# Block 2's gated delta rule: 32x32 triangular inverses by four doublings on TensorE instead of substitution in blocks of 16 on VectorE

## The chip, the cores and the metric

The kernel runs on one core of a Trainium2 chip. The metric is the device time of one execution in microseconds (us). Engines are named as in the profile: PE (TensorE, its weight loads apart as PEld), DVE (VectorE), ACT (ScalarE), POOL (GpSimd), SP (SyncE, which issues most DMAs). Each engine takes its instructions in the order of its own queue.

## The reference, cut to what matters

Two blocks follow each other. The change is in the first mixer of the second block, a chunked gated delta rule with 4 heads, 768 tokens and two directions:

```python
    a_mat = jnp.where(tri_strict, jnp.einsum('nbhid,nbhjd->nbhij', kb, kc) * decay, 0.0)
    eye = jnp.eye(cs, dtype=jnp.float32)
    t_mat = lax.linalg.triangular_solve(eye + a_mat, jnp.broadcast_to(eye, a_mat.shape),
                                        left_side=True, lower=True, unit_diagonal=True)
    u = jnp.einsum('nbhij,nbhjd->nbhid', t_mat, vb)
    w = jnp.einsum('nbhij,nbhjd->nbhid', t_mat, kb * jnp.exp(gcum)[..., None])
...
    def step(s, xs):
        u_i, w_i, qg_i, kd_i, at_i, ge_i = xs
        v_new = u_i - jnp.einsum('bhck,bhkv->bhcv', w_i, s)
        o_i = jnp.einsum('bhck,bhkv->bhcv', qg_i, s) + jnp.einsum('bhij,bhjv->bhiv', at_i, v_new)
        s = s * ge_i[..., None, None] + jnp.einsum('bhck,bhcv->bhkv', kd_i, v_new)
        return s, o_i
```

So each chunk needs the inverse of a unit triangular matrix. The kernel works in chunks of 128 tokens (6 of them), which gives 6 matrices of 128x128 for each head and direction. Beside the delta rule the same mixer has a gated MLP (`gmlp`) on the same input, and both results go through one output projection.

## The kernel before

`ab_mixer` holds the whole stage. Its big products are `dense` calls: three matmuls (`mm` or `mf` from `hh,whi`, `hl,whi` and `hh,wlo`, line L277) for each 128x128 piece of a weight, on 512 and 256 columns. The weight pieces come by DMA (`raw`) and are split by ACT (`whi`, L263) and DVE (`wlo`, L264).

The four heads run one after the other (`gdn_head`). A head first makes q, k and v by `dense`. Then `gdn_dir` runs twice, forward and backward. Each call of `gdn_dir` builds the decay-weighted matrices (L1507 on PE, L1508 and L1509 on DVE; the matrix to invert is `aT`, kept in the buffer `gkb`), calls `gdn_inv`, and then steps through 6 chunks (`gdn_chunk`: on PE L1595, L1598 and L1603, each of which waits for DVE or ACT on the step before). That makes 8 calls of `gdn_inv`.

`gdn_inv` takes the 32x32 diagonal blocks of all 6 matrices into one tile `c32` (4 blocks on the 128 partitions, 6 matrices on the free axis) and has `inv32` invert them; what follows (L1564 to L1586) joins them to 128x128 on PE. `inv32` masks the blocks to 16x16, and solves those by substitution: 15 rounds of three DVE instructions,

```python
            nc.vector.stream_shuffle(sh[:, :, W], x16[:, :, W], [j] * 16 + [16 + j] * 16)
            nc.vector.tensor_tensor(pr[:, :, W], sh[:, :, W], a[:, :, j:j + 1].broadcast_to([128, U, n]), op=ALU.mult)
            nc.vector.tensor_tensor(x16[:, :, W], x16[:, :, W], pr[:, :, W], op=ALU.subtract)
```

(L889, L890, L891). One doubling then joins two 16-blocks into a 32-block: a DVE transpose (L900), 24 small matmuls on PE (L907, `goff`), an ACT copy (L909), 24 more matmuls (L907, `gw`), a DVE subtraction (L910), and a last transpose (L911). In this text 24 such matmuls are called a piece; the trace shows each of them as two passes, so a piece is 48 rows of the trace.

`gmlp` depends on nothing of the delta rule. It is written after the heads, but a scheduler sets the order of each engine's instructions, and it puts the dense matmuls of `gmlp` (`mf`) and of the next head (`mm`) between the steps of the delta rule, and at the end those of the output projection. That order is fixed when the program is built.

After the heads, the tiles `ma` (the parts of the mixed result) come back by DMA, are multiplied by the gates (POOL, L1316), and are split into `hh` and `hl` (ACT L398, DVE L399) for the output projection.

Of the kernel before, what the change touches and what calls it, by code (L numbers as in the profile page):

```python
# [49 lines left out]
def _consts():  # L50
    p = np.arange(128)
    c = {}
# [1 line left out]
    c["bones"] = (p[:, None] // 64 == p[None, :] // 64) * 1.0  # L54
    c["ones"] = np.ones((128, 128))
    vals = [1e-5, 1e-6, 64e-5, 1e-12]
    c["m16"] = np.stack([p % 32 < 16, p % 32 >= 16], 1)
    c["i16"] = (p[:, None] % 16 == np.arange(16)[None]) * 1.0
    t32 = np.arange(32)
    for d in range(2):  # L60
        up = (p[:, None] % 32 < 16) & (t32[None] >= 16)
        c[f"off{d}"] = up if d == 0 else (p[:, None] % 32 >= 16) & (t32[None] < 16)
    c["cc"] = np.broadcast_to(np.array(vals), (128, len(vals)))
    s = p % 64
    t = np.arange(64)
    for d in range(2):
# [10 lines left out]
    s5, t5 = p[:, None] % 32, np.arange(32)[None]  # L77
# [4 lines left out]
    i = np.arange(64)  # L82
# [6 lines left out]
def _consts2():  # L89
    p = np.arange(128)  # L90
    c = {}
    t = np.arange(128)
    for d in range(2):
        le = (p[:, None] <= t[None]) if d == 0 else (p[:, None] >= t[None])
        c[f"mneg{d}"] = np.where(le, 0.0, -1e30)
        t32 = np.arange(32)
        c[f"gst{d}"] = ((p[:, None] % 32 < t32[None]) if d == 0 else (p[:, None] % 32 > t32[None])) * 1.0
    return _pack(c)


# [97 lines left out]
class B:  # L198
# [666 lines left out]
        nc.vector.transpose(flat(t), flat(x))  # L865
        return x, t

    def inv32(self, c32, U, dd, pool, pre, bank):


        nc = self.nc

        def bc(n, w):
            return self.C(n).rearrange("p (o t) -> p o t", o=1).broadcast_to([128, U, w])

        def tl(n, w, tag=None):
            return pool.tile([128, U, w], F32, tag=pre + (tag or n), name=pre + n)

        m0, m1 = self.C("m16", 0, 1), self.C("m16", 1, 2)
        off = tl("off", 32)  # L880
        nc.gpsimd.tensor_tensor(off, c32, bc(f"off{dd}", 32), op=ALU.mult)
        a, x16, sh, pr = tl("a16", 16), tl("x16", 16), tl("sh", 16), tl("pr", 16)
        nc.gpsimd.tensor_copy(x16, bc("i16", 16))
        nc.vector.tensor_scalar(a, c32[:, :, 0:16], m0, None, op0=ALU.mult)
        nc.vector.scalar_tensor_tensor(a, c32[:, :, 16:32], m1, a, op0=ALU.mult, op1=ALU.add)
        for j in (range(15, 0, -1) if dd == 0 else range(15)):
            W = slice(j, 16) if dd == 0 else slice(0, j + 1)
            n = W.stop - W.start
            nc.vector.stream_shuffle(sh[:, :, W], x16[:, :, W], [j] * 16 + [16 + j] * 16)  # L889
            nc.vector.tensor_tensor(pr[:, :, W], sh[:, :, W], a[:, :, j:j + 1].broadcast_to([128, U, n]), op=ALU.mult)  # L890
            nc.vector.tensor_tensor(x16[:, :, W], x16[:, :, W], pr[:, :, W], op=ALU.subtract)  # L891
        x = tl("x32", 32)
        nc.vector.tensor_scalar(x[:, :, 0:16], x16, m0, None, op0=ALU.mult)
        nc.vector.tensor_scalar(x[:, :, 16:32], x16, m1, None, op0=ALU.mult)
        t, w = tl("t32", 32), tl("w16", 32, "c32")
# [4 lines left out]
        nc.vector.transpose(flat(t), flat(x))  # L900
        ps = self.psum(bank, (128, 2, U, 32))
        for n in range(2):
            for u in range(U):
                for i in range(4):
                    R = slice(32 * i, 32 * i + 32)
                    l, r = (off, t) if n == 0 else (w, x)
                    nc.tensor.matmul(ps[R, n, u], l[R, u], r[R, u], start=True, stop=True, tile_position=(32 * i, 32 * i))  # L907
            if n == 0:
                nc.scalar.copy(w, ps[:, 0])  # L909
        nc.vector.tensor_tensor(x, x, ps[:, 1], op=ALU.subtract)  # L910
        nc.vector.transpose(flat(t), flat(x))  # L911
        return x, t

# [623 lines left out]
    def gdn_inv(self, aT, dd):  # L1537

        nc = self.nc
        f1 = self.f1  # L1540
        Q = [slice(32 * i, 32 * i + 32) for i in range(4)]
        c32 = f1.tile([128, 6, 32], F32, name="gc32")
        m = self.C2(f"gst{dd}").rearrange("p (o t) -> p o t", o=1).broadcast_to([128, 6, 32])
        for i in range(4):
            eng = nc.gpsimd if i % 2 else nc.vector
            eng.tensor_tensor(c32[Q[i]], aT[Q[i], :, Q[i]], m[Q[i]], op=ALU.mult)
        x, t = self.inv32(c32, 6, dd, f1, "g", "rsc")
        X = self.f2.tile([128, 6, 128], F32, name="gX")
        tn = f1.tile([128, 6, 64], F32, name="gtn")
        w = f1.tile([128, 6, 32], F32, tag="gc32", name="gw32")  # L1550
# [9 lines left out]
        ps = self.psum("rsc", (128, 2, 6, 32))  # L1560
        prs = [(2 * r + S, 2 * r + D_) for r in range(2)]
        for c in range(6):
            for s, e in prs:
                nc.tensor.matmul(ps[Q[e], 0, c], aT[Q[s], c, Q[e]], t[Q[s], c], start=True, stop=True,  # L1564
                                 tile_position=(32 * s, 32 * e))
# [215 lines left out]
```

## Time and profile before

| what | value |
|---|---|
| median of 3 runs | 2731.26 us (2726.3 to 2732.86) |
| profiled execution, its own time | 2736.78 us |
| its span, first to last instruction | 2735.0 us |
| mean granted TensorE clock | 0.947 of full |
| calls of `inv32` | 8, between 1009 and 1370 us of the span |
| the stage that holds them | 993 to 1407 us of the span |

Times inside the trace are us from the start of the span. "Busy" is the time in which an engine has an instruction running; matmuls overlap one another, so a busy PE can still be slower than its best. A granted clock of 1.00 is 2.4 GHz and 0.50 is 1.2 GHz.

### The profile page before, as it was taken

How to read it: one execution, taken by the hardware profiler on the slowest of the kernel's cores; microseconds unless marked ns; L12 is line 12 of the kernel's file. 1: busy time of each engine (PE TensorE's matmuls, PEld its weight loads, DVE VectorE, ACT ScalarE, POOL GpSimd, SP SyncE). 2: the span in 40 equal slices, each digit the busy share in tenths (PEclk: the TensorE clock that was granted, in tenths of full speed). 3: DMA queues.
4: the chain of work that ended last, by engine and by line, in shares of the span. 5: the costliest groups of instructions: out<-in, count | busy, mean ns of one | idle time of the engine just before them, and what ended most of it. 6: DMA issues, size and time to landing. Idle time of an engine off the chain costs nothing.

```text
span 2735.0 us, 53289 instructions
## 1 busy us (share of the span) xinstructions
PE 2523.7 (92%) x21320; PEld 1990.5 (73%) x21320; DVE 1621.3 (59%) x3815; ACT 1276.9 (47%) x2840; POOL 319.3 (12%) x432
## 2 busy tenths in 40 slices
PE   7989979979877989989899999999998999999998
PEld 3655646545546777777677888888886888888888
DVE  4566574576565656777856443344463767664665
ACT  3454454545455656556434332233344555542444
POOL 0121121122112000111110110011000000010010
PEclk9999989989887999999989999999998999999999
DMA  6233432434334211111231112212231102233325
GB/s 206 77 94 118 139 98 92 125 100 134 93 104 146 72 39 32 36 41 37 65 105 47 62 63 64 63 63 66 80 105 44 32 27 95 78 100 93 100 89 157
DMA packets 159016, 231.10 MB, mean 84 GB/s; under 512 B 12976, under 2 KB 90032, under 8 KB 158768
## 3 DMA queue, kind: packets, MB, share of 16 engines
q1 hardware_dynamic: 158768, 227.70, 26.7%
q8 instruction: 167, 2.74, 0.4%
q14 instruction: 81, 0.66, 0.1%
HBM read 217.95 MB, written 9.70 MB: 83 GB/s over the span
## 4 chain that ended last, share of the span: by engine, by line
PE 47%; DVE 2%; ACT 2%; issue 1%; POOL 1%; DMA 0%; POOLq 0%; SPq 0%; DVEq 0%; ACTq 0%
PE mm L277 39%; PE ms L1735 2%; PE mt L1754 1%; PE mv L351 1%; PE mt L1748 1%; PE mm L1685 1%; PE mf L277 0%; DVE hl L423 0%; DVE ht L421 0%; POOL qr L1669 0%; ACT hh L422 0%; DMA raw<-mla_w_out 0%; ACT whi L263 0%; ACT qrh L1705 0%; PE mm L1665 0%
## 5 line engine op out<-in xcount | busy, mean ns | idle before, releaser
L264 DVE TENSOR_TENSOR wlo<-raw,whi 128x512 fp32r<-128x512 f32 (+3 forms) x560 | 391.3, 701 | 395.1 <-ACT whi L263 236.6
L263 ACT CAST whi<-raw 128x512 fp32r<-128x512 f32 (+3 forms) x560 | 331.9, 594 | 462.8 <-PE mm L277 398.9
L277 PE MATMUL mm<-hh,whi 128*128 128x512 f32 (+1 forms) x1960 | 483.8, 360 | 28.0 <-ACT hh L422 13.6
L277 PE MATMUL mm<-hl,whi 128*128 128x512 f32 (+1 forms) x1960 | 457.3, 350 | 0.0
L277 PE MATMUL mm<-hh,wlo 128*128 128x512 f32 (+1 forms) x1960 | 455.3, 350 | 0.4 <-DVE wlo L264 0.4
L277 PEld LDWEIGHTS mm<-hh,whi 128*128 128x128 f32 x1960 | 332.4, 192 | 89.7 <-ACT hh L422 21.0
L277 PEld LDWEIGHTS mm<-hl,whi 128*128 128x128 f32 x1960 | 329.7, 193 | 46.8 <-issue 3.6
L277 PEld LDWEIGHTS mm<-hh,wlo 128*128 128x128 f32 x1960 | 328.9, 193 | 45.0 <-issue 2.0
L1233 POOL TENSOR_TENSOR fc<-fc,fc 128x768 f32<-128x768 f32 (+1 forms) x44 | 69.2, 1573 | 867.9 <-DVE fc L585 625.8
L277 PE MATMUL mm<-fh,whi 128*128 128x256 f32 (+1 forms) x616 | 136.3, 340 | 1.0 <-ACT fh L398 1.0
L583 DVE SCALAR_TENSOR_TENSOR fc<-mm,vec,fc 128x511 f32<-128x511 f32 (+1 forms) x132 | 86.8, 658 | 80.7 <-ACT fc L582 80.7
L277 PE MATMUL mm<-fl,whi 128*128 128x256 f32 (+1 forms) x616 | 130.5, 330 | 0.0
L277 PE MATMUL mm<-fh,wlo 128*128 128x256 f32 (+1 forms) x616 | 129.3, 328 | 0.0
L582 ACT ACTIVATE fc<-mm,vec 128x512 f32<-128x512 f32 (+1 forms) x132 | 81.4, 617 | 97.2 <-PE mm L277 97.2
L277 PEld LDWEIGHTS mm<-fh,whi 128*128 128x128 f32 x616 | 99.8, 190 | 15.8 <-issue 3.4
L318 PE MATMUL ma<-raw,cvs 128*32 128x256 f32 x832 | 95.6, 427 | 15.3 <-DMA raw<-ada_w 10.6
L277 PE MATMUL mf<-hh,whi 128*128 128x512 f32 (+1 forms) x360 | 103.6, 387 | 6.0 <-ACT whi L263 3.4
L277 PEld LDWEIGHTS mm<-fl,whi 128*128 128x128 f32 x616 | 99.0, 190 | 11.3 <-issue 0.5
L1197 DVE SCALAR_TENSOR_TENSOR xr<-mm,m,xr 128x512 f32<-128x512 f32 (+1 forms) x112 | 66.5, 597 | 67.0 <-PE mm L277 66.8
L277 PEld LDWEIGHTS mm<-fh,wlo 128*128 128x128 f32 x616 | 98.6, 190 | 10.4
L351 PE MATMUL mv<-sq,con 128*128 128x256 f32 (+1 forms) x240 | 84.3, 452 | 12.4 <-ACT sq L355 12.0
L277 PE MATMUL mf<-hl,whi 128*128 128x512 f32 (+1 forms) x360 | 95.4, 367 | 0.0
(545 smaller groups left out, 4383.6 us busy)
## 6 DMA issues: line engine op xcount, KB each, us to landing
raw<-ada_w SPq DMA_DIRECT2D x96, 512.0 KB, 4.6
raw<-ffn_up SPq DMA_DIRECT2D x176, 256.0 KB, 2.8
raw<-ffn_down SPq DMA_DIRECT2D x96, 256.0 KB, 2.7
raw<-w_in SPq DMA_DIRECT2D x66, 256.0 KB, 2.9
raw<-ab_w_in SPq DMA_DIRECT2D x50, 256.0 KB, 2.6
raw<-ffn_down SPq DMA_DIRECT2D x48, 192.0 KB, 2.4
raw<-mod_w SPq DMA_DIRECT2D x16, 512.0 KB, 7.6
raw<-w_out SPq DMA_DIRECT2D x32, 256.0 KB, 2.9
```

Of the source, the lines that this page charges most:

```text
L263: nc.scalar.copy(hi[:, :nk], raw[:, :nk])
L264: nc.vector.tensor_tensor(lo[:, :nk], raw[:, :nk], hi[:, :nk].bitcast(F32), op=ALU.subtract)
L277: nc.tensor.matmul(o, a[:, k], b[:, k0 + k, t:e], start=(k0 == 0 and j == 0 and k == 0), stop=(k0 + n == nk and j == 2 and k == n - 1))
L318: nc.tensor.matmul(acc[32 * b:32 * b + 32, c:c + 256], s[:, k, :], t[:, b], start=(k == 0), stop=(k == 7))
L351: self.nc.tensor.matmul(v[:, :x.shape[1]], self.C("ones"), x, start=(k == 0), stop=(k == 7))
L582: nc.scalar.activation(out[:, c0:c0 + cn], o[:, :cn], AF.Copy, scale=w[1])
L583: nc.vector.scalar_tensor_tensor(out[:, c0 + 1:c0 + cn], o[:, :cn - 1], w[0], out[:, c0 + 1:c0 + cn], op0=ALU.mult, op1=ALU.add)
L1197: nc.vector.scalar_tensor_tensor(x, o[:, :cn], gcol(m, 0 if c0 else 1), x, op0=ALU.mult, op1=ALU.add)
L1233: nc.gpsimd.tensor_tensor(g, g, u, op=ALU.mult)
L1685: nc.tensor.matmul(o[:, e], a[:, k, T], b[:, k], start=(i == 0), stop=(i == 5))
L1735: nc.tensor.matmul(o[:, at:at + cn], a, b, start=(j == 0), stop=(j == 4))
L1748: nc.tensor.transpose(tp[:, j], p[:, (c0 + j) * 128:(c0 + j + 1) * 128], self.C("ident"))
```

## The change

`inv32` no longer has the substitution. It starts from blocks of 2, whose inverse is the identity minus the one off-diagonal entry (two DVE instructions), and joins by doublings 2 to 4, 4 to 8, 8 to 16 and 16 to 32. Each doubling is the one that stood at the end before: transpose, piece, copy, piece, subtraction. The four off-diagonal masks are multiplied in by POOL, one tile each. `gdn_inv` no longer masks when it takes the diagonal blocks, so these are plain copies, on ACT and POOL instead of DVE and POOL. The mask tables move from the first constant table (470 to 388 columns loaded) to the second (320 to 608).

```diff
-            nc.vector.stream_shuffle(sh[:, :, W], x16[:, :, W], [j] * 16 + [16 + j] * 16)
-            nc.vector.tensor_tensor(pr[:, :, W], sh[:, :, W], a[:, :, j:j + 1].broadcast_to([128, U, n]), op=ALU.mult)
-            nc.vector.tensor_tensor(x16[:, :, W], x16[:, :, W], pr[:, :, W], op=ALU.subtract)
...
+        x, t = tl("x32"), tl("t32")
+        offs = []
+        for b in (2, 4, 8, 16):
+            o = tl(f"o{b}")
+            nc.gpsimd.tensor_tensor(o, c32, bc(f"o{b}"), op=ALU.mult)
+            offs.append(o)
+        nc.vector.tensor_tensor(x, c32, bc("n2"), op=ALU.mult)
+        nc.vector.tensor_tensor(x, x, bc("i32"), op=ALU.add)
+        w = tl("w16")
+        for o in offs:
+            nc.vector.transpose(flat(t), flat(x))
+            ps = self.psum(bank, (128, 2, U, 32))
+            for n in range(2):
+                for u in range(U):
+                    for i in range(4):
+                        R = slice(32 * i, 32 * i + 32)
+                        l, r = (o, t) if n == 0 else (w, x)
+                        nc.tensor.matmul(ps[R, n, u], l[R, u], r[R, u], start=True, stop=True, tile_position=(32 * i, 32 * i))
+                if n == 0:
+                    nc.scalar.copy(w, ps[:, 0])
+            nc.vector.tensor_tensor(x, x, ps[:, 1], op=ALU.subtract)
         nc.vector.transpose(flat(t), flat(x))
         return x, t
...
         c32 = f1.tile([128, 6, 32], F32, name="gc32")
-        m = self.C2(f"gst{dd}").rearrange("p (o t) -> p o t", o=1).broadcast_to([128, 6, 32])
         for i in range(4):
-            eng = nc.gpsimd if i % 2 else nc.vector
-            eng.tensor_tensor(c32[Q[i]], aT[Q[i], :, Q[i]], m[Q[i]], op=ALU.mult)
-        x, t = self.inv32(c32, 6, dd, f1, "g", "rsc")
+            (nc.gpsimd.tensor_copy if i % 2 else nc.scalar.copy)(c32[Q[i]], aT[Q[i], :, Q[i]])
+        x, t = self.inv32(c32, 6, lambda n: self.C2(n if n == "i32" else f"{n}{dd}"), f1, "g", "rsc")
```

The scheduler makes a new order from this. In the changed kernel's rows, lines after the edit are smaller by a few: its L275 is the old L277, its L897 is the matmul line of the doublings (old L907), its L1583, L1586 and L1591 are the chunk steps L1595, L1598 and L1603, its L1517 and L1518 are L1527 and L1528, its L396 is L398.

**First place: PE in the first call of `gdn_inv`.** Before, 87 matmuls (81 dense ones and 6 transposes of `gmlp`) stand between the last L1507 and the first piece; these are the last of them and what follows:

```order
L277 MATMUL mf<-hl,whi 128x512 x4
L277 MATMUL mf<-hh,wlo 128x512
L907 MATMUL rsc<-gt_11678,goff 32x32 x24
L277 MATMUL mf<-hh,wlo 128x512 x2
L907 MATMUL rsc<-gx_11675,gw_11679 32x32 x24
L277 MATMUL mf<-hh,wlo 128x512
L1421 MATMUL mm<-grn,con 128x512
```

Now the first piece comes after 10 dense matmuls, and three more doublings follow it:

```order
L275 MATMUL mm<-hh,wlo 128x512 x2
L897 MATMUL rsc<-gt_11622,go_11623 32x32 x24
L275 MATMUL mm<-hh,wlo 128x512 x2
L275 MATMUL mm<-hh,whi 128x512 x3
L897 MATMUL rsc<-gx_11621,gw_11633 32x32 x24
L275 MATMUL mm<-hh,whi 128x512
L275 MATMUL mm<-hl,whi 128x512 x3
L897 MATMUL rsc<-gt_11622,go_11625 32x32 x24
L275 MATMUL mm<-hl,whi 128x512
L275 MATMUL mm<-hh,wlo 128x512
L897 MATMUL rsc<-gx_11621,gw_11633 32x32 x24
L275 MATMUL mm<-hh,wlo 128x512 x3
```

The dense matmuls that stood in one run now stand between the pieces, two to five at a time. All in all 64 pieces stand where 16 stood.

**Second place: PE in the second call, while the chunk steps of the first call run.** Before, dense matmuls stand between the chunk steps:

```order
L1603 MATMUL rch<-gv_11820,gkT 128x128
L1528 MATMUL rsc<-gE,gvn 128x128
L277 MATMUL mm<-hl,whi 128x256 x3
L277 MATMUL mm<-hh,wlo 128x256
L1595 MATMUL rch<-gS,kq 128x128
L1527 MATMUL rsc<-gqg,gS 128x128
L277 MATMUL mm<-hh,wlo 128x256 x3
L1598 MATMUL rch<-gx,gX 128x128
```

Now the pieces of the doublings stand there, cut up by the chunk steps:

```order
L1583 MATMUL rch<-gS,kq 128x128
L1517 MATMUL rsc<-gqg,gS 128x128
L897 MATMUL rsc<-gt_12054,go_12055 32x32 x13
L1586 MATMUL rch<-gx,gX 128x128
L897 MATMUL rsc<-gt_12054,go_12055 32x32 x11
L1411 MATMUL mm<-grn,con 128x512
L1591 MATMUL rch<-gv_11943,gkT 128x128
L1518 MATMUL rsc<-gE,gvn 128x128
L897 MATMUL rsc<-gx_12053,gw_12065 32x32 x9
L1583 MATMUL rch<-gS,kq 128x128
L1517 MATMUL rsc<-gqg,gS 128x128
L897 MATMUL rsc<-gx_12053,gw_12065 32x32 x11
```

So a piece is entered and left more than once: the 64 pieces stand in 90 separate runs.

**Third place: ACT at the end of the stage.** Before, the splits `hh<-ma` stand in the middle of the last call's inversion:

```order
L398 CAST hh<-ma 128x512
L398 CAST hh<-ma 128x256
L398 CAST hh<-ma 128x512
L909 COPY gw_14761<-rsc 128x192
L398 CAST hh<-ma 128x256
L1555 COPY gX<-gx_14757 32x6x32 x4
```

Now they stand behind the last chunk step (L1589, before L1601), among the last gate's work (`gsg`, `gse`) and the last head's normalisation (`gon`):

```order
L1589 COPY gvn<-rch 128x128 x2
L1380 COPY gsg<-mf 128x512
L1437 ACTIVATE gon<-goa 128x768
L1380 COPY gsg<-mf 128x256
L396 CAST hh<-ma 128x512
L396 CAST hh<-ma 128x256
L344 ACTIVATE gon<-rsc,con 128x512
L344 ACTIVATE gon<-rsc,con 128x256
L335 ACTIVATE gse<-gse 128x768
L345 ACTIVATE gon<-gon 128x768
L336 ACTIVATE gse<-gse 128x768
L396 CAST hh<-ma 128x512
```

All 16 splits stand after that last step, and about 90 dense matmuls more than before follow the last head on PE.

## Rows read from the trace of the kernel before

**Rows 1.** The page, busy time by engine: us (share of the span) and instructions.

```profile
PE 2523.7 (92%) x21320; PEld 1990.5 (73%) x21320; DVE 1621.3 (59%) x3815; ACT 1276.9 (47%) x2840; POOL 319.3 (12%) x432
```

**Rows 2.** Windows, the stage: length, busy us (count) of PE PEld DVE ACT POOL, PEclk, DMA share, GB/s.

```profile
993.00:1407.00 414.00, 376.58 (x3262) 299.18 (x3262) 308.80 (x1015) 226.72 (x471) 60.88 (x74) 0.95 0.15 48
```

**Rows 3.** Waits of PE from 1000 to 1406: us in total, times, longest.

```profile
PE rsc L907 <- DVE gt L900: 7.8, 3, 4.5
...
PE mm L277 <- DVE gsh L889: 3.3, 1, 3.3
...
PE rsc L907 <- DVE gsh L889: 2.8, 1, 2.8
```

**Rows 4.** Groups of DVE instructions in the stage: busy us, mean ns, idle before.

```profile
L891 DVE TENSOR_TENSOR gx<-gx,gpr 128x6 f32<-128x6 f32 (+14 forms) x120 | 29.5, 246 | 2.6
L890 DVE TENSOR_TENSOR gpr<-gsh,ga 128x6 f32<-128x6 f32 (+14 forms) x120 | 28.0, 233 | 2.5
L889 DVE STREAM_SHUFFLE gsh<-gx 128x12 f32<-128x12 f32 (+14 forms) x119 | 25.6, 215 | 0.0
```

**Rows 5.** Timeline of PE around one piece (start, duration), and the group of L907.

```profile
1175.07 0.86 PE L277 MATMUL mm<-hh,whi 128*128 128x512 f32 x3
1175.78 0.39 PE L277 MATMUL mm<-hl,whi 128*128 128x512 f32 x1
1176.09 0.62 PE L907 MATMUL rsc<-gx,gw 32*32 32x32 f32 x48
1176.64 0.97 PE L277 MATMUL mm<-hl,whi 128*128 128x512 f32 x3
...
L907 PE MATMUL rsc<-gx,gw 32*32 32x32 f32 x384 | 5.6, 207 | 0.0
```

**Rows 6.** Timeline of the first call's doubling: first piece, ACT copy, last transpose.

```profile
1027.23 0.61 PE L907 MATMUL rsc<-gt,goff 32*32 32x32 f32 x48
...
1027.94 0.32 ACT L909 COPY gw<-rsc 128x192 f32<-128x192 f32 x1 [0.61 <-PE rsc L907]
...
1029.55 0.38 DVE L911 STREAM_TRANSPOSE gt<-gx 128x192 f32<-128x192 f32 x1
```

**Rows 7.** Timeline of the second and the eighth (last) call's doubling, first and last step.

```profile
1063.93 0.62 PE L907 MATMUL rsc<-gt,goff 32*32 32x32 f32 x48
...
1068.34 0.38 DVE L911 STREAM_TRANSPOSE gt<-gx 128x192 f32<-128x192 f32 x1
...
1366.81 0.87 PE L907 MATMUL rsc<-gt,goff 32*32 32x32 f32 x48 [4.46 <-DVE gt L900]
...
1369.65 0.38 DVE L911 STREAM_TRANSPOSE gt<-gx 128x192 f32<-128x192 f32 x1
```

**Rows 8.** Windows with a low granted clock in the stage (columns as in rows 2).

```profile
1228.50:1235.30 6.80, 6.80 (x99) 6.22 (x90) 2.29 (x5) 4.12 (x10) 0.00 (x0) 0.50 0.12 34
...
1365.00:1382.10 17.10, 13.63 (x197) 10.51 (x198) 8.30 (x19) 6.57 (x17) 3.66 (x3) 0.50 0.33 95
```

**Rows 9.** Waits of PE's weight loads from 1000 to 1406, chunk steps on DVE.

```profile
PEld rch L1598 <- DVE gx L1597: 5.9, 22, 0.7
PEld rch L1595 <- DVE gS L1605: 5.6, 17, 0.9
```

**Rows 10.** Groups of ACT instructions from 1300 to 1407, and POOL's mask in the stage.

```profile
L398 ACT CAST hh<-ma 128x512 fp32r<-128x512 f32 (+1 forms) x14 | 6.7, 511 | 3.0 <-POOL ma L1316 1.9 <-DMA ma<-gmix 1.0
...
L337 ACT ACTIVATE gse<-gse 128x768 f32<-128x768 f32 x4 | 3.4, 844 | 2.6 <-DVE gse L1391 2.6
...
L1390 ACT COPY gsg<-mf 128x256 f32<-128x256 f32 (+1 forms) x7 | 3.3, 466 | 7.4 <-issue 5.7 <-PE mf L277 1.6
...
L881 POOL TENSOR_TENSOR goff<-gc,con 128x192 f32<-128x192 f32 x8 | 4.2, 527 | 2.7 <-DVE gc L1546 2.5
```

**Rows 11.** Windows in block 1, where other small matmuls run (columns as in rows 2).

```profile
514.50:518.50 4.00, 3.21 (x132) 2.16 (x131) 3.02 (x13) 1.45 (x7) 0.44 (x2) 0.93 0.86 265
518.50:525.30 6.80, 6.49 (x131) 4.44 (x132) 2.74 (x5) 3.23 (x13) 0.20 (x1) 0.50 0.29 91
```

More of the change, by code (lines that the diff above doesn't have):

```diff
@@ L56, in _consts @@
     vals = [1e-5, 1e-6, 64e-5, 1e-12]
[L57 to L62, printed above, removed]
     c["cc"] = np.broadcast_to(np.array(vals), (128, len(vals)))
@@ L96, in _consts2 @@
         t32 = np.arange(32)
-        c[f"gst{d}"] = ((p[:, None] % 32 < t32[None]) if d == 0 else (p[:, None] % 32 > t32[None])) * 1.0
+        s5, t5 = (p[:, None] % 32, t32[None]) if d == 0 else (t32[None], p[:, None] % 32)
+        c[f"n2{d}"] = (s5 // 2 == t5 // 2) * (s5 < t5) * -1.0
+        for b in (2, 4, 8, 16):
+            c[f"o{b}{d}"] = (s5 // (2 * b) == t5 // (2 * b)) * (s5 // b < t5 // b) * 1.0
+    c["i32"] = (p[:, None] % 32 == t32[None]) * 1.0
     return _pack(c)
@@ L866, in inv8, with inv32 @@
         return x, t
-    def inv32(self, c32, U, dd, pool, pre, bank):
+    def inv32(self, c32, U, mask, pool, pre, bank):
         nc = self.nc
[L873 to L888, printed above, removed]
-            nc.vector.stream_shuffle(sh[:, :, W], x16[:, :, W], [j] * 16 + [16 + j] * 16)
-            nc.vector.tensor_tensor(pr[:, :, W], sh[:, :, W], a[:, :, j:j + 1].broadcast_to([128, U, n]), op=ALU.mult)
-            nc.vector.tensor_tensor(x16[:, :, W], x16[:, :, W], pr[:, :, W], op=ALU.subtract)
[L892 to L895, printed above, removed]
@@ L897, in flat, with bc, tl @@
+        def bc(n):
+            return mask(n).rearrange("p (o t) -> p o t", o=1).broadcast_to([128, U, 32])
+        def tl(n):
+            return pool.tile([128, U, 32], F32, tag=pre + n, name=pre + n)
         def flat(z):
             return z.rearrange("p u t -> p (u t)")
[L900 to L909, printed above, removed]
@@ L910, in inv32 @@
-        nc.vector.tensor_tensor(x, x, ps[:, 1], op=ALU.subtract)
+        x, t = tl("x32"), tl("t32")
+        offs = []
+        for b in (2, 4, 8, 16):
+            o = tl(f"o{b}")
[16 more added lines that the diff above has]
+            nc.vector.tensor_tensor(x, x, ps[:, 1], op=ALU.subtract)
```

## The prediction

> **What bounds the kernel now.** I read the page first: PE is busy for 92% of the span, no other engine for more than 59% [rows 1]. So the question is what the change does to PE. The change touches one stage, from 993 to 1407 us, and the windows of that stage are the second view: of 414 us PE is busy for 376.6, DVE for 308.8, ACT for 226.7, POOL for 60.9 [rows 2]. PE is idle for 37.4 us, about a tenth.
>
> Third, the list of waits of PE in that stage, to see what the substitution costs today. Three entries name it: pieces that wait for the transpose behind the substitution (7.8 us), pieces that wait for a shuffle of it (2.8 us), and a dense matmul that waits for a shuffle (3.3 us); 13.9 us in all [rows 3]. The other waits are for other things and stay. So the reader is to see two sizes: the substitution keeps DVE busy for 29.5 + 28.0 + 25.6 = 83.1 us [rows 4], but PE idles for only 13.9 us on its account. The scheduler has laid dense matmuls over the rest.
>
> This gives the way to count. Every matmul of the stage must be run by PE at some time. Dense matmuls that no longer hide the substitution are not saved; they stand somewhere else, between the pieces, between the chunk steps or behind the last head. So the stage's time changes by the work that PE gains, plus the waits that PE gains, less the waits that it loses.
>
> **The change, part by part.** *A, 48 more pieces.* Each call has 8 pieces where it had 2; 8 calls, 48 more. The price of a piece set among dense matmuls: a dense one of 512 columns starts at 1175.78, the piece at 1176.09, the next dense one at 1176.64, so 0.86 us from dense to dense. Without the piece the step is (1175.78 - 1175.07) / 3 = 0.24 us. A piece costs 0.62 us [rows 5], and 48 of them 29.8, say +30 us. Low end: from a piece's start to the next dense start it is 0.55 us, so 26. High end: all at half clock, 60.
>
> Here a rule speaks against the change even more. The 48 passes of that piece start within some 0.41 us (it lasts 0.62 us and a pass 0.207 us), so about 9 ns apart [rows 5]. The Trainium skill, TensorE: Matmul & The Clock Gate, "Wait — 56ns, not 53.3ns?", says that matmuls never start closer than about 25 ns, however few columns they have. By that page a piece would be 48 x 25 ns = 1.2 us and its switch, the 48 pieces some 67 us, and the whole sum some 37 us higher. The trace does not agree for these pieces, which spread over four tiles of the array; the sum goes by the row.
>
> *B, pieces that are cut.* The 64 pieces stand in 90 runs, so PE enters and leaves small matmuls 26 more times. Entering costs 1176.09 - 1175.78 - 0.24 = 0.07 us. Leaving: the last pass starts at 1176.09 + 0.62 - 0.21 = 1176.50, the next dense one at 1176.64, 0.14 us [rows 5]. 26 x 0.21 is +5 us; ends: 0, and the price of a whole piece each, 16.
>
> *C, new waits inside the doublings.* From the first piece's start to the end of the transpose, the doubling of the first call took 1029.55 + 0.38 - 1027.23 = 2.70 us, with nothing in its way [rows 6]; that of the second call 4.79 us, that of the eighth 3.22 us [rows 7]. The eight lie between these ends, half of them above 3.2. In most of the new doublings the order gives PE two pieces, two dense matmuls while ACT copies, and four while DVE subtracts and transposes: 2 x 0.62 + 6 x 0.24 = 2.7 us. So PE waits for 0 to 2.1 us in each; I take 3.2 - 2.7 = 0.5, since most rows are near 3.2: 24 x 0.5 = +12 us; ends 0 and 24 x 2.1 = 50. Behind a late piece the chunk steps and dense matmuls of the same queue wait too, which is in this term. The first piece of a call now waits for two copies, one mask and three DVE instructions; ten dense matmuls, 2.4 us, stand ahead of it. I cost that at nothing; if that cover is too short, it is 8 waits of up to 2.1 us, 17.
>
> *D, waits that go:* the substitution's, -14 us [rows 3]; nothing else of PE waits for it by name.
>
> *E, the end of the stage.* Once the last head is done, PE has only the output projection, and for that it needs all the splits. Before, these lay inside the last call. Now ACT has behind the last chunk step: 16 splits of 0.51 us on average, 5 passes over 768 columns (the gate, the normalisation) of 0.84, and two copies of 0.47 [rows 10], 13.3 us together. PE has meanwhile the last two normalisation matmuls and the part of the projection that the first four tiles allow, 12 x 0.24 + 12 x 0.12 = 4.3 us; with the former some 5.6 us. That leaves 7.7 us; the first copies lie beside the last dense ones, so I take +6 us, between 0 and 14.
>
> *F, the clock.* Two stretches of the stage ran at 1.2 GHz right after long waits of pieces: at 1228.5 (6.80 us, PE busy throughout) and at 1365.0 (17.10 us, PE busy for 13.63), the latter around the 4.46 us wait for the last call's transpose [rows 7, 8]. At 2.4 GHz that work would take half, so they cost 3.4 + 6.8 = 10.2 us. With the waits gone I give back all of it, -10 us; ends -10 and 0.
>
> *G, chunk steps.* PE's weight loads for L1598 and L1595 wait for DVE for 5.9 + 5.6 = 11.5 us [rows 9], and the substitution is 83.1 of DVE's 308.8 us [rows 2, 4], 27%. I give back that share, -3 us; ends 0 and -11.5.
>
> *At nothing:* POOL gains three masks of 0.53 us a call [rows 10], 12.6 us; it is busy for 60.9 of 414 [rows 2], and each mask is made while the doubling before it (2.7 us) runs. If that cover went, each call would be late by up to 1.6 us, 13 us in all. ACT's three more copies a call are the 0.32 us inside C [rows 6]. The larger mask table is 0.15 MB at the head of the stage, under dense matmuls; uncovered, at the stage's 48 GB/s [rows 2], it is 3 us.
>
> Sum: 30 + 5 + 12 - 14 + 6 - 10 - 3 = **+26 us**. Against the profiled execution that is 2736.8 + 26 = 2763 us. That execution lies 5.5 us above the median of the three runs, 2731.3, so for the median I say **2757 us**.
>
> **The rivals.** *The chain is the bound, and it gets faster.* DVE loses most of 83 us, and what PE waits for may have been DVE's queue everywhere: then C, B and E come to nothing (the pieces fall into places where PE would have waited), G is whole, and A is at its low end: 26 - 14 - 10 - 11.5 = -9.5, so 2722 us. For it: DVE is busy for three quarters of the stage, and in the last head the wait for the transpose was exposed (4.46 us). Against: 91% of the stage PE is busy, and pieces are work for PE. It decides where B, C and E together stay under about 3 us.
>
> *Nothing to measure.* Only B, C and E come to nothing and the rest is as forecast: 30 - 14 - 10 - 3 = +3, so 2734 us. The doublings would have to be as quick as the first row of them, 2.70 us, nearly always; one of the three shown was.
>
> *The clock falls in the doublings.* In block 1, in the 4 us before 518.5, PE was busy for 3.21 us, nearly all of it matmuls on a part of the array, and then the granted clock fell to 0.50 for 6.8 us [rows 11]. In the changed stage 32 doublings of 3.4 us are 109 us in which almost half of PE's time goes to small pieces. If a quarter of that ran at half clock, it costs 14 us, and F is not given back: 26 + 14 + 10 = +50, so 2781 us. Against: the doublings of the trace run among dense matmuls, and the low stretches of rows 8 came after waits.
>
> **How the numbers follow.** The forecast has a chance of 0.5, the quick chain 0.2, no change 0.15, the clock 0.15. A change of less than 0.3% (8 us) can hardly be told from none. Faster is the quick chain, 0.2; within 0.3% the second rival, 0.15; slower the forecast and the clock, 0.65. The forecast's own range is 2740 to 2775, from C between 0 and twice its value and F between its ends. The range for 8 in 10 reaches down to the quick chain's 2722 and up to 2786, the clock's case with some of C's upper end.
>
> **What would show it.** Right: in the stage PE's busy time grows by about 35 us and its length by somewhat less; no wait of PE for a shuffle is left, and pieces wait for the ACT copy and for the transpose in short waits of about 0.5 us; DVE's busy time falls by some 80 us while the time gets no shorter; after the last head PE waits for `hh` splits. Wrong: PE's idle time in the stage falls well under 20 us, or a piece among dense matmuls costs much less than 0.62 us. What would break the sum most is C, whose ends are 50 us apart, and the clock.

## The result and the profile after

The changed kernel takes 2751.05 us (median of 4 runs, 2749.99 to 2753.35) against 2730.56 us before (4 runs, 2726.3 to 2732.86): 1.0078 times as long, 95% interval 1.0061 to 1.0095, that is 17 to 26 us. The profiled execution took 2753.35 us, with a span of 2751.6 us.

The page of the changed kernel, its line of busy time (columns as in [rows 1]):

```profile
PE 2554.8 (93%) x23624; PEld 2014.5 (73%) x23624; DVE 1565.7 (57%) x3351; ACT 1286.3 (47%) x2880; POOL 331.3 (12%) x448
```

PE has 31 us more to do than in [rows 1], DVE 56 less. For the stage the two traces must be laid over each other at the same instructions. In this execution block 1, whose instructions are the same in both kernels, was 10.8 us shorter, so the stage starts at 993 - 10.8 = 982.2; everything behind the stage stands 16.9 us later, so its end, 1407 before, is 1423.9. The windows of the changed kernel, first the stage, then the four doublings of the first call (columns as in [rows 2]):

```profile
982.20:1423.90 441.70, 414.92 (x5566) 326.00 (x5565) 260.72 (x561) 239.58 (x518) 76.03 (x92) 0.95 0.15 48
...
1001.00:1012.84 11.84, 11.84 (x418) 9.05 (x419) 3.77 (x9) 4.51 (x9) 1.00 (x2) 1.00 0.02 4
```

The stage grew by 27.7 us: PE's busy time by 414.92 - 376.58 = 38.3 us, while its idle time fell from 37.4 to 26.8. In the first call's doublings PE is busy for all of 11.84 us, at full clock. The timeline of PE there shows why (start, duration):

```profile
1001.00 0.61 PE L897 MATMUL rsc<-gt,go 32*32 32x32 f32 x48
1001.54 0.73 PE L275 MATMUL mm<-hh,wlo 128*128 128x512 f32 x2
1002.11 0.86 PE L275 MATMUL mm<-hh,whi 128*128 128x512 f32 x3
1002.90 0.62 PE L897 MATMUL rsc<-gx,gw 32*32 32x32 f32 x48
1003.45 0.50 PE L275 MATMUL mm<-hh,whi 128*128 128x512 f32 x1
1003.79 0.87 PE L275 MATMUL mm<-hl,whi 128*128 128x512 f32 x3
1004.59 0.62 PE L897 MATMUL rsc<-gt,go 32*32 32x32 f32 x48
```

Between the pieces shown stand five and four dense matmuls, and they last at least as long as the copy or the subtraction and transpose that the next piece needs. The price of a piece is read here again: from 1002.11 to 1003.45 run three dense ones and one piece, 1.34 - 3 x 0.24 = 0.62 us.

Two dense matmuls behind the first piece of a doubling and four behind the second, as the prediction counted them, stand in the fifth call:

```profile
1208.69 0.62 PE L897 MATMUL rsc<-gt,go 32*32 32x32 f32 x48
1209.24 0.73 PE L275 MATMUL mm<-hl,whi 128*128 128x512 f32 x2
1209.90 0.62 PE L897 MATMUL rsc<-gx,gw 32*32 32x32 f32 x48
1210.45 1.19 PE L275 MATMUL mm<-hh,wlo 128*128 128x512 f32 x4
1211.57 0.62 PE L897 MATMUL rsc<-gt,go 32*32 32x32 f32 x48
```

From doubling to doubling that is 2.88 us, with no wait of PE between.

The list of waits of PE from 1000 to 1424 us (total, times, longest), the answer to [rows 3]:

```profile
PE mm L275 <- DVE hl L397: 4.3, 2, 3.4
PE mm L275 <- ACT hh L396: 3.6, 2, 3.1
PE mf L275 <- DVE sgu L1368: 3.6, 3, 2.3
PE rsc L1559 <- DVE gw L1555: 3.1, 5, 1.8
...
PE rch L1591 <- ACT gvn L1589: 1.9, 3, 0.9
...
PE rsc L897 <- issue: 0.5, 1, 0.5
...
PE rsc L897 <- ACT gw L899: 0.4, 1, 0.4
```

No wait for a shuffle is left; the stage has no shuffle any more. Pieces (L897) wait hardly at all. At the top stand the splits `hh` and `hl` behind the last head. DVE's groups of the doublings in the stage (columns as in [rows 4]) show what replaced its 83.1 us of substitution:

```profile
L890 DVE STREAM_TRANSPOSE gt<-gx 128x192 f32<-128x192 f32 x32 | 12.1, 377 | 0.9
L900 DVE TENSOR_TENSOR gx<-gx,rsc 128x192 f32<-128x192 f32 x32 | 11.3, 352 | 40.6 <-PE rsc L897 38.1 <-ACT whi L261 2.1
```

### The profile page after: what moved, and what is told of

Same layout as the page of the kernel before. It is cut to its first block, busy times and chain, and to the rows that moved or that the text cites. A ratio compares the mean times of both kernels' runs of the same rounds, so it can differ in the third digit from the quotient of the medians.

```text
span 2751.6 us, 57559 instructions
## 1 busy us (share of the span) xinstructions
PE 2554.8 (93%) x23624; PEld 2014.5 (73%) x23624; DVE 1565.7 (57%) x3351; ACT 1286.3 (47%) x2880; POOL 331.3 (12%) x448
## 4 chain that ended last, share of the span: by engine, by line
PE 76%; DVE 11%; ACT 7%; issue 3%; DMA 2%; POOL 1%; SPq 0%; POOLq 0%; DVEq 0%; ACTq 0%
PE mm L275 48%; PE mf L275 6%; PE mv L349 3%; PE ms L1723 2%; PE ma L316 1%; PE rsc L897 1%; PE mt L1742 1%; PE rsc L1497 1%; PE mt L1736 1%; DMA raw<-ada_w 1%; DVE wlo L262 1%; PE mm L1673 1%; DVE hl L421 1%; PE rsc L859 1%; PE rsc L761 1%
## 5 line engine op out<-in xcount | busy, mean ns | idle before, releaser
L262 DVE TENSOR_TENSOR wlo<-raw,whi 128x512 fp32r<-128x512 f32 (+2 forms) x560 | 387.7, 695 | 397.3 <-ACT whi L261 240.5
L261 ACT CAST whi<-raw 128x512 fp32r<-128x512 f32 (+2 forms) x560 | 331.5, 594 | 480.9 <-PE mm L275 397.2
L275 PE MATMUL mm<-hh,whi 128*128 128x512 f32 (+1 forms) x1960 | 483.8, 360 | 22.2 <-ACT hh L420 13.6
L275 PE MATMUL mm<-hl,whi 128*128 128x512 f32 (+1 forms) x1960 | 457.2, 349 | 4.3 <-DVE hl L397 4.3
L275 PE MATMUL mm<-hh,wlo 128*128 128x512 f32 (+1 forms) x1960 | 455.7, 350 | 0.0
L275 PEld LDWEIGHTS mm<-hh,whi 128*128 128x128 f32 x1960 | 331.9, 192 | 84.5 <-ACT hh L420 21.1
L275 PEld LDWEIGHTS mm<-hl,whi 128*128 128x128 f32 x1960 | 328.0, 192 | 51.9 <-DVE hl L397 5.5
L275 PEld LDWEIGHTS mm<-hh,wlo 128*128 128x128 f32 x1960 | 327.7, 192 | 44.7 <-issue 2.0
L275 PE MATMUL mm<-fh,whi 128*128 128x256 f32 (+1 forms) x616 | 136.2, 339 | 1.0 <-ACT fh L396 1.0
L275 PE MATMUL mm<-fl,whi 128*128 128x256 f32 (+1 forms) x616 | 130.5, 330 | 0.0
L275 PE MATMUL mm<-fh,wlo 128*128 128x256 f32 (+1 forms) x616 | 129.3, 328 | 0.0
L275 PEld LDWEIGHTS mm<-fh,whi 128*128 128x128 f32 x616 | 99.8, 189 | 15.8 <-issue 3.4
L275 PE MATMUL mf<-hh,whi 128*128 128x512 f32 (+1 forms) x360 | 103.5, 385 | 6.9 <-DVE sgu L1368 3.6
L275 PEld LDWEIGHTS mm<-fl,whi 128*128 128x128 f32 x616 | 98.9, 190 | 11.3 <-issue 0.5
L275 PEld LDWEIGHTS mm<-fh,wlo 128*128 128x128 f32 x616 | 98.6, 190 | 10.4
L275 PE MATMUL mf<-hl,whi 128*128 128x512 f32 (+1 forms) x360 | 98.1, 371 | 0.0
L275 PE MATMUL mf<-hh,wlo 128*128 128x512 f32 (+1 forms) x360 | 97.1, 370 | 0.5 <-DVE wlo L262 0.5
```

The source lines that it names most:

```text
L261: nc.scalar.copy(hi[:, :nk], raw[:, :nk])
L262: nc.vector.tensor_tensor(lo[:, :nk], raw[:, :nk], hi[:, :nk].bitcast(F32), op=ALU.subtract)
L275: nc.tensor.matmul(o, a[:, k], b[:, k0 + k, t:e], start=(k0 == 0 and j == 0 and k == 0), stop=(k0 + n == nk and j == 2 and k == n - 1))
```

## The experiments

Stated before the runs: the theory is that a piece is work for PE wherever it stands, and that the substitution cost what PE waited for it. The rivals are that the pieces fall into time in which PE would have waited, and that the chain from piece to piece is what PE waits for. In the table, time and ratio to the kernel before are of runs on the same chip. The stage is the same stretch of the program in each profile; its idle time is length less PE's busy time, and "clock" is the granted clock in it. "At half" is the part of PE's busy time that lies in stretches with a granted clock of 0.50. "Work" is an estimate of what the busy time would be at full clock: busy time less 0.43 of the part at half, since 49 matmuls that took 10.20 us at half clock took 5.85 at full (the two kernels again, below). So a stage's length is its work, 0.43 of "at half", and its idle time. The four profiles with 16 pieces stand at 359 to 365 us of work, so the estimate is good to some 6 us.

| kernel | pieces | median us | ratio, 95% interval | stage us | PE busy | at half | work | PE idle | clock |
|---|---|---|---|---|---|---|---|---|---|
| before | 16 | 2730.56 | 1 | 414.0 | 376.6 | 40.5 | 359.2 | 37.4 | 0.95 |
| before, again | 16 | 2731.88 (one run) | | 414.0 | 376.7 | 40.5 | 359.2 | 37.3 | 0.95 |
| changed | 64 | 2751.05 | 1.0078 (1.0061 to 1.0095) | 441.7 | 414.9 | 37.1 | 399.0 | 26.8 | 0.95 |
| changed, again | 64 | 2750.94 | 1.0084 (1.0065 to 1.0103) | 435.1 | 408.2 | 22.0 | 398.7 | 26.9 | 0.96 |
| one doubling | 16 | 2716.96 | 0.9956 (0.9941 to 0.997) | 404.9 | 376.7 | 26.8 | 365.2 | 28.2 | 0.95 |
| five doublings | 80 | 2756.37 | 1.0101 (1.0081 to 1.012) | 441.5 | 418.0 | 13.6 | 412.2 | 23.5 | 0.98 |
| blocks of 8 | 32 | 2738.64 | 1.0036 (1.0022 to 1.005) | 424.4 | 390.3 | 31.9 | 376.6 | 34.1 | 0.96 |
| blocks of 4 | 48 | 2737.84 | 1.0031 (1.002 to 1.0043) | 424.7 | 399.1 | 19.9 | 390.5 | 25.6 | 0.97 |
| gmlp between | 64 | 2779.47 | 1.0183 (1.0163 to 1.0202) | 461.6 | 420.7 | 45.5 | 401.1 | 40.9 | 0.94 |
| slower chain | 64 | 2767.23 | 1.0148 (1.0125 to 1.0172) | 452.9 | 421.6 | 45.6 | 402.0 | 31.3 | 0.95 |
| half the passes | 64 | 2753.33 | 1.0087 (1.0064 to 1.011) | 434.7 | 406.8 | 25.2 | 396.0 | 27.9 | 0.96 |
| extra pieces, before | 64 | 2821.87 | 1.0337 (1.0322 to 1.0353) | 511.3 | 443.6 | 138.7 | 384.0 | 67.7 | 0.84 |
| extra pieces, after | 96 | 2777.66 | 1.0183 (1.0164 to 1.0201) | 465.0 | 435.4 | 36.9 | 419.5 | 29.7 | 0.96 |
| both directions | 16 | 2741.66 | 1.0058 (1.0039 to 1.0078) | 429.2 | 384.7 | 50.0 | 363.2 | 44.5 | 0.93 |

The work column follows the pieces: from 16 (one doubling) over 32, 48 and 64 to 80 it is 365, 377, 390, 399 and 412 us, some 0.73 us a piece. The sums over the stretches at half clock (columns as in [rows 2]) are, for before (seven, from 1088.5, 1119.2, 1194.3, 1228.5, 1317.2, 1330.9 and 1365.0), changed (six, from 1064.3, 1118.9, 1187.2, 1293.0, 1361.2 and 1398.8), changed again (four) and extra pieces before (twelve):

```profile
sum 44.36, PE 40.53 PEld 32.51 DVE 19.87 ACT 19.39 POOL 3.62; mean PE 5.79 PEld 4.64 DVE 2.84 ACT 2.77 POOL 0.52
sum 44.38, PE 37.11 PEld 29.50 DVE 24.14 ACT 19.98 POOL 15.34; mean PE 6.19 PEld 4.92 DVE 4.02 ACT 3.33 POOL 2.56
sum 30.73, PE 21.97 PEld 16.56 DVE 20.27 ACT 16.23 POOL 13.20; mean PE 5.49 PEld 4.14 DVE 5.07 ACT 4.06 POOL 3.30
sum 160.44, PE 138.67 PEld 109.45 DVE 52.64 ACT 44.81 POOL 9.80; mean PE 11.56 PEld 9.12 DVE 4.39 ACT 3.73 POOL 0.82
```

**One doubling.**

```diff
-        for b in (2, 4, 8, 16):
+        for b in (16,):
```

> The changed kernel with the doublings 2 to 4, 4 to 8 and 8 to 16 left out (48 of the 64 pieces gone; the inverses are then not those of the reference). Theory, pieces are work for PE: the 48 pieces and their switches go, 48 x 0.62 + 26 x 0.21 = 35 us, with some 3 us of waits inside the doublings, so about 2751 - 38 = 2713 us, and PE's busy time in the stage falls by some 35 us. Rival, pieces fall into places where PE would have waited and the loss sits in the end of the stage and in the clock: the time falls by less than 12 us, to 2740 to 2750, and PE's idle time in the stage grows instead. Against the kernel before, this run is also what the substitution cost there as a whole: 14 us of waits would give 2717, with the clock and DVE's share returned 2704.

Measured 2716.96, close to the theory's 2713. From this run to the changed kernel PE's busy time in the stage rises by 414.92 - 376.68 = 38.2 us, the work by 34, and its idle time falls by 1.4: the pieces are work, not filling. Against the kernel before it is 12.7 us shorter, with the same busy time and 9.2 us less idle time: that is what taking the substitution out was worth, with the new order and the other masks that come with it.

**Five doublings.**

```diff
+        oz = tl("oz")
+        nc.gpsimd.memset(oz, 0.0)
+        offs.append(oz)
```

> The changed kernel with a fifth doubling in each call, with an off-diagonal tile of zeros, so that the inverse stays the same: 16 more pieces. Theory, pieces are work for PE: 16 x 0.62 + 9 x 0.21 = 12 us, with a wait or two 13, so about 2764 us. Rival, pieces fall into places where PE would have waited: 2751 to 2755 us. Second rival, the chain from piece to piece is what PE waits for: 8 calls x 3.2 us, 2776 us.

Measured 2756.37: between the theory and its first rival, and the chain as the only bound is out. The step from the changed kernel is 6 us give or take some 7 (by the two intervals), so the time alone does not part the theory from that rival. The window of the stage (columns as in [rows 2]) does:

```profile
986.40:1427.90 441.50, 418.04 (x6331) 325.95 (x6330) 264.75 (x577) 240.14 (x522) 75.33 (x99) 0.98 0.15 47
```

The granted clock is 0.98 here, not 0.95: only 13.6 us of PE's busy time lie at half clock, against 37.1 and 22.0 in the changed kernel. The work rose by 13 us for 16 pieces, as the theory says, and the clock gave most of it back. Over the whole program the clock was 0.955 to 0.958 in five of the six executions and 0.947 in one, and that one took 2768.32 us. Why it stayed higher in this kernel is not shown.

**Blocks of 8, blocks of 4.** Substitution in smaller blocks, with two or three doublings; the core of both edits:

```diff
-        nc.vector.tensor_tensor(x, c32, bc("n2"), op=ALU.mult)
-        nc.vector.tensor_tensor(x, x, bc("i32"), op=ALU.add)
+        nc.vector.tensor_tensor(x, c32, bc("db"), op=ALU.mult)
...
+        nc.vector.reduce_sum(a, x.rearrange("p u (j t) -> p u t j", t=B), axis=mybir.AxisListType.X)
+        for j in (range(B - 1, 0, -1) if dd == 0 else range(B - 1)):
...
+            nc.vector.stream_shuffle(sh[:, :, W], xb[:, :, W], [B * b + j for b in range(32 // B) for _ in range(B)])
...
```

> Substitution in blocks of 8 (7 rounds of three DVE instructions) and two doublings: 32 pieces where the kernel before has 16 and the changed one 64. Theory, pieces are work for PE and the substitution cost only its waits: 16 more pieces than before, +10, switches +2, waits -10 (the chain on DVE is half as long, and 13.9 us is all there is), DVE's share -2: 2731 us, between 2724 and 2738, and 20 us below the changed kernel. Rival, DVE's queue holds the chunk steps up more than the waits by name show: 2710 to 2720 us. Rival, waits of the substitution stay as they were since some rounds remain: 2742 us.

> Substitution in blocks of 4 (3 rounds) and three doublings, 48 pieces: the size between the run with blocks of 8 (2738.6) and the changed kernel (2751). Theory, pieces are work for PE: the changed kernel less 16 pieces, 0.65 us and some switches each, 11 to 12 us, with 1 or 2 us of waits for the rounds given back: 2739 to 2743 us. Rival, a substitution of any length costs its waits on DVE while doublings cost little: 2750 us or more.

Blocks of 8 took 2738.64: just over the 2738 that the theory allowed, and nearer to its second rival, 2742. PE still waits 3.8 us for shuffles there, in this row of its list of waits:

```profile
PE rsc L910 <- DVE gsh L895: 3.8, 4, 1.8
```

Before, the waits that name the substitution came to 13.9 us [rows 3], so the step "waits -10" came true. What went wrong is that the idle time fell by only 3.3 us: other waits grew, those for the splits `hh` and `hl` to 3.0 + 2.0 us from 1.1, for `gx` to 2.2 from 0.2. Blocks of 4 came out just under the 2739 to 2743 of the theory, 13 us below the changed kernel with 16 pieces less. Neither beats the kernel before.

**gmlp between the calls.**

```diff
-            for _ in gd:
-                pass
+            for n, _ in enumerate(gd):
+                if n >= 0:
+                    next(gm, None)
```

> The changed kernel with the parts of gmlp written between the calls of gdn_dir instead of after the heads; the same instructions in another order, and the splits for the output projection then stand before the last chunk steps on ACT. Theory, the end of the stage costs some 7 us of waits for hh and hl and a stretch at half clock there costs up to 7 more: 2738 to 2745 us. Rival, the dense matmuls of gmlp are then used up early and pieces of the last calls wait: 2751 us or more.

Measured 2779.47: the rival, and 28 us above the changed kernel. The waits of PE in the stage:

```profile
PE rsc L897 <- DVE gt L890: 4.6, 4, 1.5
...
PE rsc L897 <- ACT gw L899: 2.7, 6, 0.5
```

Now the doublings of the last two calls have no dense matmuls between their pieces, and every step of the chain shows. The work is that of the changed kernel within 2 us; PE's idle time rose by 14. The waits for `hh` fell to 1.9 us, and it did not pay.

**The two kernels again.**

> The kernel before, profiled once more: no edit. It shows how far block 1, whose instructions are the same in all kernels of this study, and the low-clock stretches differ from one execution to another. In the first profile the last split of a weight piece ahead of the stage stood at 972.6 us, in the changed kernel at 961.8. If those 10.8 us are chance, this profile falls anywhere from 960 to 973 with more or less of the clock low ahead of it; if they come from the smaller constant table, it stands near 972 again. The stage itself should take 466 us within some 5.

> The changed kernel, profiled and timed once more: no edit. 2751 us; the stage some 493 us long within 5, and block 1 as in the run before it. If the low-clock stretches of the stage stand at the same places again, they come from the order; if elsewhere, they are not a term that can be put down to the change.

(The 466 and 493 us count the stage from the last split of a weight piece ahead of it; in the stage of this text they are 414 and 441.7.) The kernel before: its stage is the same to a tenth of a us, with the low-clock stretches at the same places, and it starts 4.8 us earlier, so the start differs from one execution to the next. The changed one: four of its six low-clock stretches stand at the same places, and the stage is 6.6 us shorter, more than the 5 expected. Two low-clock stretches are gone, one of 3.4 us at 1293.0 and one of 10.2 us. The windows of the latter and of the last one, first profile:

```profile
1361.20:1371.40 10.20, 10.20 (x49) 8.17 (x47) 1.62 (x4) 2.96 (x5) 1.83 (x1) 0.50 0.32 103
1398.80:1412.50 13.70, 9.43 (x26) 6.93 (x27) 12.96 (x13) 5.39 (x15) 9.09 (x5) 0.50 0.25 73
```

and again, first the same 49 matmuls, then the low-clock stretch:

```profile
1363.00:1368.85 5.85, 5.85 (x49) 4.69 (x47) 1.63 (x4) 2.77 (x5) 1.82 (x1) 1.00 0.30 112
1395.10:1408.80 13.70, 8.89 (x25) 6.51 (x25) 12.61 (x11) 5.39 (x14) 10.13 (x5) 0.50 0.25 72
```

The first piece of work came once at half and once at full clock, and took 10.20 and 5.85 us; the second, in which the splits keep PE waiting, came both times at half.

**Slower chain.**

```diff
+        xd = tl("xd")
         for o in offs:
-            nc.vector.transpose(flat(t), flat(x))
+            nc.vector.tensor_copy(xd, x)
+            nc.vector.tensor_copy(x, xd)
+            nc.vector.tensor_copy(xd, x)
+            nc.vector.transpose(flat(t), flat(xd))
```

> The changed kernel with three more DVE copies of 128x192 in front of each of the 32 transposes inside the doublings, so that the chain from piece to piece gets longer by 3 x 0.25 to 0.35 us each time, and PE's work stays the same. Theory, PE's work bounds the stage and the chain is hidden under dense matmuls: 2751 to 2759 us, PE's busy time in the stage unchanged. Rival, the chain is what PE waits for: 32 x 0.75 to 1.05 = 24 to 34 us, 2775 us or more.

Measured 2767.23, between the two: the chain is not free to grow. Of the 24 to 34 us added to it some 16 came out, although PE's idle time is only 4.5 us above that of the changed kernel and the work only 3 us; the rest is that more of PE's busy time stood at half clock, 45.6 us against 37.1 and 22.0. These copies also take DVE's time (282.69 us busy in the stage, 22 more), and the chunk steps wait for DVE too. Which of the two did it stays open.

**Half the passes.**

```diff
-                for u in range(U):
+                for u in range(0, U, 2):
...
-                        nc.tensor.matmul(ps[R, n, u], l[R, u], r[R, u], start=True, stop=True, tile_position=(32 * i, 32 * i))
+                        nc.tensor.matmul(ps[R, n, u:u + 2], l[R, u], r[R, u:u + 2], start=True, stop=True, tile_position=(32 * i, 32 * i))
```

> The changed kernel with every second small matmul left out and the others taken over 64 columns instead of 32 (matrices 1, 3 and 5 are multiplied by the weights of 0, 2 and 4, so the inverses are not those of the reference): half as many passes over the same columns. If a piece costs by its passes, about 9 ns each, 64 x 24 x 9 ns = 14 us go and the time is 2737 us. If it costs by its columns, nothing goes: 2751 us. If it costs mostly by being entered and left, also 2751.

Measured 2753.33: nothing went. The timeline has one of these pieces as

```profile
1010.33 0.54 PE L897 MATMUL rsc<-gx,gw 32*32 32x64 f32 x24
```

0.54 us instead of 0.62, so a pass of 64 columns takes half as long again as one of 32, and the 64 pieces save 5 us, less than these runs can tell from nothing. That a pass costs 9 ns whatever its columns is out: half the passes over twice the columns are only a little cheaper. How the rest is shared between columns, entering and leaving is not shown.

**Extra pieces.** In the kernel before, behind the subtraction; the other run has one such piece in each doubling, with `o` for `off`:

```diff
+        for _ in range(6):
+            for u in range(U):
+                for i in range(4):
+                    R = slice(32 * i, 32 * i + 32)
+                    nc.tensor.matmul(ps[R, 0, u], off[R, u], off[R, u], start=True, stop=True, tile_position=(32 * i, 32 * i))
```

> The kernel before with six more pieces in each call, behind its one doubling; they read only the off-diagonal mask tile, nothing reads what they write, and the substitution stays: PE's work of the change without its chain. In the order they stand as one run of 144 matmuls in each call, so they are not entered and left anew. Theory, pieces are work for PE wherever they stand: 48 x 0.43 = 21 us, so 2749 us. Rival, PE has room for them in its waits: under 2735 us.

> The changed kernel with one more piece in each of the 32 doublings that nothing waits for (it reads the off-diagonal tile alone, and nothing reads what it writes): PE gets 32 more pieces, the chain from piece to piece stays as it is. Theory, PE's work bounds the stage: 32 x 0.43 to 0.65 = 14 to 21 us, 2765 to 2772 us. Rival, the chain bounds the stretches in which the doublings stand, and PE has room there: 2751 to 2756 us.

The second gave 2777.66, 27 us above the changed kernel: PE has no room for them. In the profile the stage grew by 23.3 us, 20.5 of it work, within the theory's 14 to 21, and 2.9 idle time. The first gave 2821.87, 92 us above the kernel before, where 21 was expected. The rival (room in the waits) is out. Of the 97 us by which the profiled stage grew only 25 are work, near the theory's 21; 30 are idle time, and 42 come of 138.7 us of PE's busy time at half clock instead of 40.5. The trace shows where these come from, in the waits of PE and in the windows around the first such run of matmuls:

```profile
PE rsc L915 <- issue: 25.7, 14, 2.5
```

```profile
1029.00:1032.80 3.80, 1.68 (x170) 1.46 (x160) 0.00 (x0) 2.30 (x6) 0.00 (x0) 1.00 0.02 4
1032.80:1049.90 17.10, 15.15 (x224) 12.13 (x225) 3.74 (x9) 1.98 (x5) 0.41 (x1) 0.50 0.01 2
```

After 170 passes PE stands still for 2.5 us and waits for nothing that the profile names; then the clock is at half for 17.1 us while PE is busy for 15.15. That comes back in nearly every call; what PE waits for is taken up in the last section. In the run behind the changed kernel, where two pieces often stand next to each other, such waits add up to 7.7 + 3.1 us:

```profile
PE rsc L897 <- issue: 7.7, 9, 1.7
...
PE rsc L904 <- issue: 3.1, 5, 1.0
```

**Both directions in one substitution.** In the kernel before, 12 matrices at once:

```diff
+        prep = [self.gdn_dir(h, dd, kq) for dd in range(2)]
+        x, t = self.gdn_inv2([p[0] for p in prep])
         for dd in range(2):
-            self.gdn_dir(h, dd, kq, kT, vT, oa)
...
+            self.gdn_run(h, dd, kq, kT, vT, oa, xt, *prep[dd])
```

> The kernel before with the substitution of both directions of a head in one: the blocks of the backward direction are transposed, so that 12 matrices go through the same 15 rounds, four times instead of eight (60 rounds instead of 120; the one doubling then has 48 matmuls in a piece instead of 24, as many in all). The run with one doubling and no substitution stood at 2717 us, 12 below the kernel before; that is what can be had. Theory, the substitution costs where the chain of its rounds leaves PE without work, and half as many chains cost half as much: 2729 - 6 = 2723 us, between 2719 and 2728. Rival, the first direction now waits for the products of the second and for rounds that are twice as wide, and the two directions' chunk steps have no inversion between them to be laid over: 2730 to 2740 us.

Measured 2741.66: the rival, a little above its range. The waits that name the substitution did fall, from 13.9 to 2.9 us, but PE's waits moved to the chunk steps and to gmlp:

```profile
PE rch L1623 <- ACT gvn L1621: 6.7, 7, 2.2
PE mf L1345 <- ACT av L1339: 4.6, 2, 2.7
PE mf L1361 <- ACT vt L1346: 3.9, 1, 3.9
```

No version tried with the whole computation beats the kernel before.

## Why the prediction came out right, and where its terms were off

The forecast was +26 us, 2757; the median rose by 20.5, in the second comparison by 23.8 (2750.94 against 2727.17), and the profiled stage by 27.7 and 21.1. The sign and the mechanism (pieces are work for PE) were right. Of the terms, C was too high, and F gave back too much in the first profile; that the two nearly cancel there, so that the sum came so near, is luck.

- **A and B, pieces and switches, +35.** PE's busy time in the stage rose by 38.3 us (31.6 in the second profile), its work by 40 in both, and by 34 from one doubling to four. In time that last step costs 34 us, 0.71 us a piece. Right. What a switch costs was not measured by itself.
- **C, waits inside the doublings, +12.** Wrong by most of it: pieces wait for 1.1 us (0.5 and 0.4 shown above, 0.2 for POOL). The step that failed is the 3.2 us taken as a doubling's usual length. Six dense matmuls to a doubling is right for the fifth call, and there doubling follows doubling in 2.88 us with no wait of PE; so it runs at the 2.70 us of [rows 6] and some 0.2 us to the next piece. The 3.22 us of the last call [rows 7] had been measured in a stretch at half clock [rows 8], where a piece took 0.87 us. By the prices above the matmuls of such a doubling need 2.68 us; the 0.2 us left would be a wait that counts as busy time, at most some 5 us over the 24 doublings (an estimate). The run with the slower chain shows that little is to spare.
- **D, waits that go, -14.** Gone by name. With the pieces held equal, in the run with one doubling, idle time fell by 9.2 us, since that run has 7.5 us of waits for the splits as well.
- **E, the end of the stage, +6.** 4.3 + 3.6 us of waits for `hl` and `hh`, against 1.1 before: +6.8. Right. What it leaves out is the stretch at half clock around these waits, 13.7 us with PE busy for 9.43, which is another 4 us.
- **F, the clock, -10.** Wrong in the first profile, nearly right in the second, and not for its reason. [rows 8] show two of seven low-clock stretches, 44.4 us in all, with 40.5 us of PE's busy time in them. Those two are gone, but others came: the changed stage has 44.4 us at half clock with PE busy for 37.1 in the first profile, 30.7 with 22.0 in the second. At 0.43 that gives back 1.5 and 8 us. Over the whole program the clock was 0.951 on average in 10 executions of the changed kernel, 0.949 in 50 of the kernel before, less than it differs between executions of one kernel (0.947 to 0.953).
- **G, chunk steps, -3.** The weight loads' waits of [rows 9] fell from 11.5 to 7.0 us, PE's own waits for `gvn`, `gx` and `gS` by about 2. Right. The two rows now:

```profile
PEld rch L1586 <- DVE gx L1585: 3.8, 13, 0.7
PEld rch L1583 <- DVE gS L1593: 3.2, 14, 0.6
```

- **At nothing.** POOL's busy time rose by 15 us, and hardly any wait of PE names it. Right.

With what was measured (work, C, D, E, G by PE's own waits, F) the first profile's sum is 40 + 1 - 14 + 7 - 2 - 1.5 = 30 us, against 27.7; the second's is 24, against 21.1. Of the marks in the last part of the prediction, PE's busy time, the missing shuffle waits and the splits came as said. DVE's busy time fell by 48 us, not 80. Not taken off were its 24 more subtractions and 24 more transposes (24 x 0.73 = 17.5 us) and the two instructions that make the first blocks (8 us). The masks that went too (some 25 us) would make up for these; but the splits `hl` and the products `gE` took 10 us longer than before, and the records of other DVE instructions had overlapped those of the substitution by 18 us, which busy time counts once. Why the splits and products took longer is not shown. Of the rivals, the quick chain had the waits of the doublings right (there are hardly any), but the work of PE outweighs that. The second one's condition, doublings about as quick as the first row, came true as well; it fell because the switches and the end of the stage cost what the forecast said. The clock rival fell: no piece of the stage ran in a low-clock stretch.

The whole profiled spans differ by only 16.6 us because block 1 was 10.8 us shorter. That is chance: in the 14 profiles the stage starts anywhere within some 11 us, and for the kernel before 4.8 us apart.

## What to carry to other kernels

On an engine that is busy for nine tenths of a stage, moving work onto it costs the work itself, and moving it away from another engine gives back little more than the waits: 83 us of DVE's time were worth 12.7 us here. Before small matmuls are added, read their price between dense ones, entering and leaving included (0.62 us, 0.71 measured), and check that dense ones remain to stand between them. And look at idle time and clock together: in the table the kernels with most idle time of PE (67.7, 44.5, 40.9 us) have the lowest clock (0.84, 0.93, 0.94), those with least (23.5, 25.6) the highest (0.98, 0.97).

## What the runs showed of the hardware that was not expected

- A run of 144 small matmuls (288 passes) stops PE. In the run with extra pieces it waited 25.7 us in 14 such places, with no semaphore named. The Trainium skill, Runtime: NRT & Kernel Launch, "Instruction fetch mechanics", says that an engine's instructions are fetched ahead in blocks of 256 and that crossing a block is mostly hidden. The rows of one queue of instructions, in the stage before and with extra pieces (packets, MB, share of 16 engines), show 18 packets more; the stage has 4608 PE instructions more (48 passes and 48 weight loads in each of 48 pieces), which is 256 to a packet, so the trace agrees with the first part:

```profile
q8 instruction: 26, 0.43, 0.4%
q8 instruction: 44, 0.72, 0.6%
```

  Each of the 14 waits, and each of two more at the next matmuls (L1569), ended 1.26 to 1.54 us after a packet of this queue was through; in the run with extra pieces behind the changed kernel 15 of 16 waits that name nothing ended 1.19 to 1.54 us after one. So these are waits for instructions, as far as their times can tell, and "mostly hidden" does not hold for passes this short.
- Small matmuls between dense ones kept the full clock (1.00 in the 11.84 us of the first call's doublings); the same ones in one run were followed by 17.1 us at 0.50.
- Passes of 32 columns that go round four tiles start (0.62 - 0.20) / 47 = 9 ns apart, those of 64 columns (0.54 - 0.22) / 23 = 14 ns apart.
